# Split weight tiles in two phases of 128 bytes, in a hybrid decoder trunk in float32

## The chip, the cores and the metric

The kernel runs on one core of one Trainium2 chip, as one program in one launch. The metric is the time of one execution in microseconds (us). The core has a matrix engine (TensorE, "PE" in the profile, with its weight loads shown apart as "PEld"), a vector engine (VectorE, DVE), a scalar engine (ScalarE, ACT), GpSimd (POOL), a queue processor (SyncE, SP) that issues most of the loads, 128 partitions of on-chip memory in which every tile lives, and eight accumulator banks that TensorE writes.

## The reference

Two layers act on 256 rows of width 1024. Each layer is a half-step FFN, a token mixer beside four memory cross-attention heads, and another half-step FFN. The mixer of layer 0 is a chunkwise mLSTM, that of layer 1 a sliding-window attention.

```python
def swiglu(x, w_in, w_out):
    gate, up = jnp.split(x @ w_in, 2, axis=-1)
    return (jax.nn.silu(gate) * up) @ w_out
...
    mem_kv = rms_norm(mem, mem_norm_g) @ mem_w_kv
...
    for i in range(DEPTH):
        j = i // N_MIXERS
        x = x + 0.5 * swiglu(rms_norm(x, ffn1_norm_g[i]), ffn1_w_in[i], ffn1_w_out[i])
        hn = rms_norm(x, mix_norm_g[i])
        if i % N_MIXERS == 0:
            proj = hn @ a_w_in[j]
            y_tok = mlstm_heads(proj[..., :A_TOK], a_gate_b[j], a_h_norm_g[j])
...
        y_mem = memory_heads(xq, mem_k, mem_v, xa_q_norm_g[i], xa_k_norm_g[i])
        x = x + jnp.concatenate([y_tok, y_mem], axis=-1) @ w_out
        x = x + 0.5 * swiglu(rms_norm(x, ffn2_norm_g[i]), ffn2_w_in[i], ffn2_w_out[i])
    return x
```

D_MODEL is 1024, the FFN's inner width 2816. All is float32, and nearly all the work is in the products with the weights.

## The kernel before

**Products in three parts.** Each weight tile and each activation is split into a high part, rounded to the matmul's float32r, and the low part that is left over. A product is then three matmuls into one accumulator bank: high by high, high by low, low by high (`mm3`, line 449). All of them go through the helper `mm` (line 445), so that the profile shows nearly every matmul on line 446. Each is 128 by 128 weights against 256 moving columns.

**The weight stream.** The class `Stream` (line 266) brings the weights in the order of one long plan, tile after tile, 349 of them. Tile i goes through three steps. `fetch` issues the load into a raw tile `wr`, `round` (line 290) has ScalarE copy it to the high tile `wh` in float32r (line 300), and `rest` (line 303) has VectorE subtract to get the low tile `wl` (line 315). TensorE takes a tile with `take` and gives it back with `drop`. Most tiles are 128 partitions by 1024 elements, 4096 bytes in a partition. The tile pools are rings: `wrp` has 5 buffers, `whp` and `wlp` have 8 each, so tile i reuses the buffer of tile i - 8.

**The stages.** `program()` runs `memory`, `ffn`, `mixer_a`, `ffn`, `ffn`, `mixer_b`, `ffn`. One FFN has 11 groups of four weight tiles for its inner columns, and 24 tiles for its output; a tile serves 24 matmuls, and the FFN has 1,584. In its first part the moving operands are `xh` and `xl`, the split activations; in the second they are tiles `u`, the split hidden columns. The weights are the stationary operand there. Some projections of the mixers (groups with `rows=True`) do it the other way: `xh` and `xl` are stationary, and `wh` and `wl` move. `Norm.finish` (line 527) sums the squares of a row with two matmuls on the constant tile `onesr` (four, on a norm with `rows=False`); they stand on line 446 too, between the matmuls of the next stage. Transposes (line 460) and the small products of the heads (lines 455, 1366, 1371, 1422) interrupt the stream only in the mixers.

**The order.** It is written out while the program is built: `Weave` keeps a clock for each engine and decides when each step is issued. No address enters into it.

**Addresses.** The pools lie one behind the other in a partition, in the order in which they are made, and a pool takes the size of its tiles. The constants of `cst` come first, so the first pool behind them, `xhp`, begins at byte 29,632. From the sizes follow these places (bytes in a partition) and their phase, the place modulo 512; every tile in a ring and every slice that a matmul takes lies a multiple of 512 bytes further:

| tiles | first byte | modulo 512 |
|---|---|---|
| `onesr` | 16,512 | 128 |
| `xh`, `xl` | 29,632 and 37,824 | 448 |
| `u` | 46,016 | 448 |
| `wr` | 113,664 | 0 |
| `wh` | 134,144 | 0 |
| `wl` | 166,912 | 0 |
| `t` | 199,680 | 0 |

In what follows, the distance of a matmul is the place of its stationary operand less that of its moving one, modulo 512. It is (0 - 448) = 64 for all matmuls on weight tiles in the FFNs and output projections, 448 - 0 = 448 for the row-wise groups, 128 - 448 = 192 for `Norm.finish` with `onesr` stationary, and 448 - 128 = 320 where `onesr` moves. The low tile of a weight lies 32,768 bytes behind its high tile.

Of the kernel before, what the change touches and what calls it, by code (L numbers as in the profile page):

```python
# [10 lines left out]
F32 = mybir.dt.float32  # L11
F32R = mybir.dt.float32r
# [7 lines left out]
P = 128  # L20
# [120 lines left out]
def tile_trunk(ctx: ExitStack, tc: tile.TileContext, a, out):  # L141
# [3 lines left out]
    def mk(pool, shape, dt, tag):  # L145
        seq[0] += 1
        return pool.tile(shape, dt, tag=tag, name=f"{tag}_{seq[0]}")

    def pool(name, bufs, **kw):
        return ctx.enter_context(tc.tile_pool(name=name, bufs=bufs, **kw))  # L150

    cst = pool("cst", 1)
    onesr = mk(cst, [P, T], F32R, "onesr")
    nc.vector.memset(onesr.bitcast(F32), 1.0 / D)
    wv = Weave()


    xhp = pool("xhp", 4)
# [1 line left out]
    up = pool("up", 31)  # L160
    vp = pool("vp", 2)
    wrp = pool("wrp", 5)
    whp = pool("whp", 8)
    wlp = pool("wlp", 8)
    tp = pool("tp", 8)
    sp = pool("sp", 2)
    gp = pool("gp", 1)
    cp = pool("cp", 24)
    pbs = [pool(f"pb{i}", 1, space=PSUM) for i in range(8)]

    tt = nc.vector.tensor_tensor
# [56 lines left out]
    maskd = con[:, C_MASK:C_MASK + T]  # L228
    ones = mk(cst, [P, 1], F32, "ones")
    nc.vector.memset(ones, 1.0)  # L230
    mhalf = mk(cst, [P, 16], F32, "mhalf")
    nc.vector.memset(mhalf, -0.5)
    warm = mk(cst, [P, 1], F32, "warm")
    act(warm, ones, AF.Silu)
# [31 lines left out]
    class Stream:  # L266
# [23 lines left out]
        def round(self, i):  # L290
            shape, j = self.plan[i][1], Job(wv, self.landed[i])
            gates = shape[2] == 8
            n = 1024 if gates else shape[1] * shape[2]
            self.hi[i] = mk(whp, [P, 8, P] if gates else shape, F32R, "wh")
            if gates:
                nc.gpsimd.memset(self.hi[i].bitcast(F32), 0.0)
                for s in range(2):
                    nc.scalar.copy(self.hi[i][:, :, s * 32:s * 32 + 4], self.raw[i][:, :, s * 4:s * 4 + 4])
            else:
                nc.scalar.copy(self.hi[i], self.raw[i])  # L300
            self.cast[i] = j.act(n)

        def rest(self, i):
            shape, j = self.plan[i][1], Job(wv, self.cast[i])
            gates = shape[2] == 8
            self.lo[i] = mk(wlp, [P, 8, P] if gates else shape, F32R, "wl")
            if gates:
                nc.gpsimd.memset(self.lo[i].bitcast(F32), 0.0)
                for s in range(2):
                    d = slice(s * 32, s * 32 + 4)  # L310
                    tt(out=self.lo[i][:, :, d], in0=self.raw[i][:, :, s * 4:s * 4 + 4],
                       in1=self.hi[i][:, :, d].bitcast(F32), op=ALU.subtract)
                j.dve(64)
            else:
                tt(out=self.lo[i], in0=self.raw[i], in1=self.hi[i].bitcast(F32), op=ALU.subtract)  # L315
                j.dve(shape[1] * shape[2])
            self.subbed[i] = j.t
# [100 lines left out]
    def mixer_plan(w, pair, rest, w_out, gates=None):  # L418
        for kh in range(2):
            for c0 in pair:  # L420
                yield cols(w, c0, kh)
        for c0 in rest:
            if c0 == gates:
                yield chunks(w)[:, :, c0:c0 + 8], [P, 8, 8], None
                continue
            for kh in range(2):
                yield cols(w, c0, kh)
        for kc in ORDER + LATE:
            yield row(w_out, kc)
# [1069 lines left out]
```

## Time and profile before

| | |
|---|---|
| three timed runs | 1007.48, 1008.93, 1001.01 us; median 1007.48 |
| the profiled execution | 1016.15 us |
| its span, first to last instruction | 1014.3 us |
| granted TensorE clock, mean | 0.997 |
| moved by the DMA engines | 182.72 MB, mean 180 GB/s |

The page's span is the time between the first and the last instruction of one execution; the execution's own time is 1.85 us longer. The profiled execution is the longest of the four. Busy times are sums over one engine. A matmul's recorded duration is modelled, and the next one starts before it ends: what the engine does per unit of time is read from the starts, or from the number of matmuls in a window.

### The profile page before, as it was taken

The numbers are of one execution on the slowest core, as the hardware profiler recorded it, in microseconds if no ns is written. First come the engines' busy times: TensorE is split into PE (matmuls) and PEld (weight loads), VectorE is DVE, ScalarE is ACT, GpSimd is POOL, SyncE is SP. The second block draws the span as 40 slices with busy tenths as digits, with TensorE's granted clock in tenths as the row PEclk, the third lists the DMA queues.
The fourth block names the chain that finished last, engine by engine and source line by source line (L and its number), as shares of the span: only waits on it lengthen the run. The fifth ranks groups of instructions, "written<-read, shape, count | busy, mean of one in ns | idle before, by whom it ended". The sixth has DMA issues, their size and how long they took to land.

```text
span 1014.3 us, 20574 instructions
## 1 busy us (share of the span) xinstructions
PE 1004.9 (99%) x8554; PEld 989.9 (98%) x8554; DVE 677.9 (67%) x1096; ACT 512.9 (51%) x774; POOL 56.9 (6%) x46
## 2 busy tenths in 40 slices
PE   8999999999999999999999999999999999999998
PEld 7999999999999999999999999999998899999998
DVE  6985565668766596655567667665778778666551
ACT  6754453456556465444444445354566665453440
POOL 1400000010101000000010000000111010000000
PEclk9999999999999999999999999999999999999999
DMA  8876545656454666665656665656622347656650
GB/s 287 251 230 201 192 157 179 205 154 191 124 183 141 191 187 195 196 205 165 199 165 183 212 209 168 194 191 190 214 85 83 102 150 246 211 176 203 200 170 23
DMA packets 171614, 182.72 MB, mean 180 GB/s; under 512 B 7196, under 2 KB 165328, under 8 KB 171520
## 3 DMA queue, kind: packets, MB, share of 16 engines
q1 hardware_dynamic: 170384, 179.60, 56.3%
q8 instruction: 67, 1.10, 0.4%
q0 software_dynamic: 416, 0.75, 0.4%
q10 hardware_dynamic: 720, 1.05, 0.3%
q14 instruction: 27, 0.22, 0.1%
HBM read 180.32 MB, written 1.05 MB: 179 GB/s over the span
## 4 chain that ended last, share of the span: by engine, by line
PE 98%; DMA 1%; DVE 0%; SPq 0%; ACT 0%; issue 0%; DVEq 0%
PE bank L446 93%; PE bank L455 2%; PE bank L460 2%; DMA wr<-in_mem_w_kv_dram 1%; PE bank L1371 1%; PE bank L1422 1%; PE bank L1366 0%; ACT wh L300 0%; SPq L376 0%; DVE t L865 0%; DVE wl L315 0%; DVE t L866 0%; SPq L287 0%; DVEq L315 0%
## 5 line engine op out<-in xcount | busy, mean ns | idle before, releaser
L315 DVE TENSOR_TENSOR wl<-wr,wh 128x1024 fp32r<-128x1024 f32 (+2 forms) x349 | 407.3, 1206 | 52.9 <-ACT wh L300 52.2
L446 PE MATMUL bank<-xh,wh 128*128 128x256 f32 x1544 | 431.6, 280 | 0.0
L446 PE MATMUL bank<-xh,wl 128*128 128x256 f32 x1544 | 430.6, 279 | 0.0
L446 PE MATMUL bank<-xl,wh 128*128 128x256 f32 x1544 | 430.6, 279 | 0.0
L300 ACT CAST wh<-wr 128x1024 fp32r<-128x1024 f32 (+2 forms) x349 | 341.0, 1020 | 77.7 <-PE bank L446 53.1
L446 PE MATMUL bank<-u,wh 128*128 128x256 f32 x1792 | 313.0, 280 | 0.0
L446 PEld LDWEIGHTS bank<-xh,wh 128*128 128x128 f32 x1544 | 291.6, 189 | 0.1
L446 PEld LDWEIGHTS bank<-xh,wl 128*128 128x128 f32 x1544 | 291.6, 189 | 0.0
L446 PEld LDWEIGHTS bank<-xl,wh 128*128 128x128 f32 x1544 | 290.0, 188 | 0.1
L446 PEld LDWEIGHTS bank<-u,wh 128*128 128x128 f32 x1792 | 271.9, 188 | 1.7 <-issue 1.7
L446 PE MATMUL bank<-u,wl 128*128 128x256 f32 x896 | 249.9, 279 | 0.0
L446 PEld LDWEIGHTS bank<-u,wl 128*128 128x128 f32 x896 | 169.2, 189 | 0.0
L797 ACT ACTIVATE t<-t 128x512 f32<-128x512 f32 x44 | 27.8, 632 | 192.2 <-DVE t L794 191.8
L794 DVE TENSOR_TENSOR t<-bank,rb 128x256 f32<-128x256 f32 x88 | 36.7, 424 | 86.2 <-PE bank L446 86.2
L446 PE MATMUL bank<-wh,xh 128*128 128x256 f32 x208 | 60.0, 289 | 0.0
L520 POOL TENSOR_TENSOR u<-u,t 128x512 f32<-128x512 f32 x14 | 24.5, 1750 | 606.0 <-ACT t L517 605.8
L494 ACT ACTIVATE xh<-u,gcol 128x256 fp32r<-128x256 f32 x48 | 21.7, 502 | 72.5 <-DVE u L847 59.9
L446 PE MATMUL bank<-wl,xh 128*128 128x256 f32 x208 | 57.9, 279 | 0.0
L446 PE MATMUL bank<-wh,xl 128*128 128x256 f32 x208 | 57.9, 278 | 0.0
L844 DVE TENSOR_TENSOR t<-bank,hrb 128x512 f32<-128x512 f32 x15 | 10.4, 691 | 64.3 <-PE bank L446 64.3
L800 DVE TENSOR_TENSOR t<-t,bank 128x256 f32<-128x256 f32 x88 | 33.1, 418 | 27.0 <-ACT t L797 26.9
L466 DVE TENSOR_TENSOR u<-t,u 128x512 fp32r<-128x512 f32 x44 | 30.4, 692 | 28.2 <-ACT u L464 28.2
(189 smaller groups left out, 657.4 us busy)
## 6 DMA issues: line engine op xcount, KB each, us to landing
wr<-in_ffn_w_in_dram SPq DMA_DIRECT2D x176, 512.0 KB, 5.0
wr<-in_ffn_w_out_dram SPq DMA_DIRECT2D x80, 512.0 KB, 4.9
wr<-in_a_w_in_dram SPq DMA_DIRECT2D x28, 512.0 KB, 4.5
wr<-in_b_w_in_dram SPq DMA_DIRECT2D x14, 512.0 KB, 4.9
wr<-in_a_w_out_dram SPq DMA_DIRECT2D x12, 512.0 KB, 4.3
wr<-in_b_w_out_dram SPq DMA_DIRECT2D x12, 512.0 KB, 3.2
wr<-in_ffn_w_out_dram SPq DMA_DIRECT2D x16, 256.0 KB, 2.6
wr<-in_mem_w_kv_dram SPq DMA_DIRECT2D x6, 512.0 KB, 8.0
```

What stands on the lines that cost most here:

```text
L300: nc.scalar.copy(self.hi[i], self.raw[i])
L315: tt(out=self.lo[i], in0=self.raw[i], in1=self.hi[i].bitcast(F32), op=ALU.subtract)
L446: nc.tensor.matmul(ps, lhsT, rhs, start=start, stop=stop, skip_group_check=True)
L455: nc.tensor.matmul(ps, lhsT, rhs, start=start, stop=stop, skip_group_check=True)
L460: nc.tensor.transpose(ps, src, ident[:k, :k])
L466: tt(out=lo, in0=src, in1=hi.bitcast(F32), op=ALU.subtract)
L494: act(hi[:, m], xn[:, m], AF.Copy, scale=g(self.gi + 2 * c2 + m))
L520: nc.gpsimd.tensor_tensor(out=self.acc, in0=self.acc, in1=sq, op=ALU.add)
L794: tt(out=t[:, m], in0=bs[m].t[:, :T], in1=x.rb, op=ALU.mult)
L797: act(t, t, AF.Silu)
L800: tt(out=t[:, m], in0=t[:, m], in1=bs[m].t[:, T:], op=ALU.mult)
L844: tt(out=t, in0=halves(b.t), in1=pair(x.hrb), op=ALU.mult)
```

## The change

The ring of eight high tiles becomes two rings of four, and so does the ring of eight low tiles. Tile i goes to ring i modulo 2. Between the first and the second pair of rings the pool `gp` is put, which held one tile of 64 bytes (`acol`) and now also holds `mhalf`, another 64 bytes: together 128. `mhalf`, a constant that GpSimd's power operations read (line 473), leaves the constants for that, and a tile `pad` of the same size is put among them, so that the pools behind them begin where they did.

```diff
     wv = Weave()
+    mk(cst, [P, 16], F32, "pad")
...
-    whp = pool("whp", 8)
-    wlp = pool("wlp", 8)
+
+    whp, wlp = [pool("whp0", 4)], [pool("wlp0", 4)]
+    gp = pool("gp", 1)
+    whp.append(pool("whp1", 4))
+    wlp.append(pool("wlp1", 4))
     tp = pool("tp", 8)
     sp = pool("sp", 2)
-    gp = pool("gp", 1)
     cp = pool("cp", 24)
+    mhalf = mk(gp, [P, 16], F32, "mhalf")
...
-    mhalf = mk(cst, [P, 16], F32, "mhalf")
...
-            self.hi[i] = mk(whp, [P, 8, P] if gates else shape, F32R, "wh")
+            self.hi[i] = mk(whp[i % 2], [P, 8, P] if gates else shape, F32R, f"wh{i % 2}")
...
-            self.lo[i] = mk(wlp, [P, 8, P] if gates else shape, F32R, "wl")
+            self.lo[i] = mk(wlp[i % 2], [P, 8, P] if gates else shape, F32R, f"wl{i % 2}")
```

The places after it, from the sizes:

| tiles | first byte | modulo 512 |
|---|---|---|
| `wh0`, `wl0` (even tiles) | 134,144 and 150,528 | 0 |
| `mhalf`, `acol` | 166,912 and 166,976 | |
| `wh1`, `wl1` (odd tiles) | 167,040 and 183,424 | 128 |
| `t` | 199,808 | 128 |

`onesr`, `xh`, `xl`, `u` and `wr` stay where they were; some small constants move by 64 bytes, and `t` and the small pools behind it by 128 (`cp`, the last, by 64). A tile is still reused after eight. For an odd tile the distance is 192 in place of 64, and 320 in place of 448 in the row-wise groups; for an even tile it is as before. A low tile lies 16,384 bytes behind its high tile. Of the program's matmuls in float32r, about half work on odd tiles.

## The prediction

> **What bounds the kernel now.** I read the page first: the span, the busy shares, the granted clock and the chain of work that ended last.
>
> ```profile
> span 1014.3 us, 20574 instructions
> PE 1004.9 (99%) x8554; PEld 989.9 (98%) x8554; DVE 677.9 (67%) x1096; ACT 512.9 (51%) x774; POOL 56.9 (6%) x46
> PEclk9999999999999999999999999999999999999999
> PE 98%; DMA 1%; DVE 0%; SPq 0%; ACT 0%; issue 0%; DVEq 0%
> L315 DVE TENSOR_TENSOR wl<-wr,wh 128x1024 fp32r<-128x1024 f32 (+2 forms) x349 | 407.3, 1206 | 52.9 <-ACT wh L300 52.2
> L300 ACT CAST wh<-wr 128x1024 fp32r<-128x1024 f32 (+2 forms) x349 | 341.0, 1020 | 77.7 <-PE bank L446 53.1
> ```
>
> TensorE is 98% of the chain, at full clock. The cast and the subtraction that split a weight tile take 1.02 and 1.21 us on two engines that are 51% and 67% busy, so they stand off the path. What counts is the rate at which TensorE takes matmuls. A matmul's own duration does not tell it, since neighbours overlap; the distance from start to start, which I call the pitch, does. So I asked next how many matmuls of line 446 (the helper `mm`) fall into the whole span and into the four FFNs (columns: window, its length, TensorE busy and matmuls, weight loads, granted clock, DMA share, GB/s):
>
> ```profile
> 0.00:1014.30 1014.30, 956.59 (x8154) 948.21 (x8154) 1.00 0.57 180
> 49.60:228.20 178.60, 178.60 (x1518) 178.60 (x1518) 1.00 0.61 188
> 362.00:547.80 185.80, 185.80 (x1579) 185.80 (x1579) 1.00 0.62 193
> 548.20:727.50 179.30, 179.30 (x1585) 179.30 (x1584) 1.00 0.62 193
> 838.10:1009.00 170.90, 170.90 (x1511) 170.90 (x1510) 1.00 0.57 179
> ```
>
> The second and third FFN run the same code on the same shapes at the same clock and DMA share, yet one takes 185.8 us for 1,579 matmuls and the other 179.3 us for 1,585. The view of one line, cut to a stretch inside the first, second, third and fourth FFN, shows it again (one kind of matmul, every third of the stream; durations min/median/max, first and last start):
>
> ```profile
> L446 PE MATMUL bank<-xh,wh x279: 280/281/282, 59.7 to 158.0; 128*128 128x256 f32 x140
> L446 PE MATMUL bank<-xh,wh x306: 280/281/282, 369.7 to 477.5; 128*128 128x256 f32 x153
> L446 PE MATMUL bank<-xh,wh x295: 275/276/277, 560.0 to 659.9; 128*128 128x256 f32 x148
> L446 PE MATMUL bank<-xh,wh x293: 275/276/277, 849.8 to 949.1; 128*128 128x256 f32 x147
> ```
>
> (158.0 − 59.7) us / 278 / 3 = 117.9 ns and (477.5 − 369.7) / 305 / 3 = 117.8 ns; (659.9 − 560.0) / 294 / 3 = 113.3 ns and (949.1 − 849.8) / 292 / 3 = 113.4 ns. There are two pitches, a long one of 117.8 and a short one of 113.3, 4.5 ns apart, and a stage keeps the one it begins with from its first tile to its last. Weight loads show the same two cases (first FFN, then third):
>
> ```profile
> L446 PEld LDWEIGHTS bank<-xh,wh x278: 191/192/193, 60.0 to 157.8; 128*128 128x128 f32 x139
> L446 PEld LDWEIGHTS bank<-xh,wh x295: 187/188/188, 559.9 to 659.8; 128*128 128x128 f32 x148
> ```
>
> Under the long pitch one load of three lasts 192 ns, under the short one all last 188.
>
> **What one pitch or the other is worth.** Counting in the timeline from start to start, 4,103 of the 8,112 neighbouring pairs of line 446 stand at 116 to 126 ns: the two FFNs above (3,097) and about a thousand in the opening and the mixers. 4,103 × 4.5 ns = 18.5 us. The profiled execution took 1016.15 us (span 1014.3 and 1.85 around it), so with the short pitch throughout it would be 997.7 us, and with the long one throughout 997.7 + 8,154 × 4.5 ns = 1034.4 us. On this scale the three timed runs hold about 9% (1001.01), 27% (1007.48) and 31% (1008.93) of long pitch, the profiled one 50%; one whole FFN is 1,584 × 4.5 ns = 7.1 us, about the step between the timed runs. I take it, as an estimate, that the runs of before differ by which stages fell into which pitch.
>
> **What sets the pitch.** The trace has a few places where the address distance between weights and moving operand changes without a pause. In an FFN the moving tiles stand at 448 and the weights at 0 in 512 bytes, a distance of 64. The sum of squares (`Norm.finish`, two matmuls on `onesr`, which stands at 128) sits between FFN tiles and makes it 192 for two matmuls: exactly the distance that the odd tiles get after the change. The timeline of TensorE at the end of the second FFN, and at the start of that same FFN (start us, duration, matmul):
>
> ```profile
> 547.70 0.28 PE L446 MATMUL bank<-xh,wl 128*128 128x256 f32 x1
> 547.82 0.40 PE L446 MATMUL bank<-u,onesr 128*128 128x256 f32 x2
> 548.06 0.28 PE L446 MATMUL bank<-xh,wh 128*128 128x256 f32 x1
> 548.17 0.28 PE L446 MATMUL bank<-xl,wh 128*128 128x256 f32 x1
> 548.29 0.28 PE L446 MATMUL bank<-xh,wl 128*128 128x256 f32 x1
> 548.40 0.28 PE L446 MATMUL bank<-xh,wh 128*128 128x256 f32 x1
> ```
> ```profile
> 361.44 0.28 PE L446 MATMUL bank<-xl,wh 128*128 128x256 f32 x1
> 361.55 0.28 PE L446 MATMUL bank<-xh,wl 128*128 128x256 f32 x1
> 361.67 0.46 PE L446 MATMUL bank<-u,onesr 128*128 128x256 f32 x2
> 361.96 0.28 PE L446 MATMUL bank<-xh,wh 128*128 128x256 f32 x1
> 362.08 0.28 PE L446 MATMUL bank<-xl,wh 128*128 128x256 f32 x1
> 362.20 0.28 PE L446 MATMUL bank<-xh,wl 128*128 128x256 f32 x1
> ```
>
> In the first, long pitch comes in and short pitch leaves, for the whole third FFN. In the second, short comes in (0.11 apart) and long leaves (0.12), for the whole second FFN. The timeline has the first kind four times (at 46, 228, 548 and 838 us) and the second once, there with a pause of some 60 ns inside. So a trip 64, 192, 64 turned the pitch over in five cases of five. The row-wise projections of the mixers, whose moving operand is the weight tile, stand at 448, and 320 on `onesr`; there are two more turns:
>
> ```profile
> 727.47 0.28 PE L446 MATMUL bank<-wh,xl 128*128 128x256 f32 x1
> 727.58 0.64 PE L446 MATMUL bank<-onesr,u 128*128 128x256 f32 x4
> 728.05 0.28 PE L446 MATMUL bank<-wh,xh 128*128 128x256 f32 x1
> 728.17 0.28 PE L446 MATMUL bank<-wl,xh 128*128 128x256 f32 x1
> ```
> ```profile
> 256.85 0.28 PE L446 MATMUL bank<-wh,xl 128*128 128x256 f32 x1
> 256.96 0.28 PE L446 MATMUL bank<-xh,wh 128*128 128x256 f32 x1
> 257.08 0.28 PE L446 MATMUL bank<-xl,wh 128*128 128x256 f32 x1
> 257.20 0.28 PE L446 MATMUL bank<-xh,wl 128*128 128x256 f32 x1
> ```
>
> From 448 to 320, short becomes long at once; from 448 to 64 too. What neither trace nor code shows is a long stretch at 192 or 320.
>
> **The change part by part.** It adds and removes no instruction: engine by engine the two programs have the same operations, shapes and waits in the same order, and each split tile is still reused after eight. Moving `mhalf` changes where 31 small POOL operations read; POOL is 6% busy: nothing. Casts and subtractions may run at other speeds at the new addresses: 1.02 and 1.21 us against the 24 × 113.3 ns = 2.7 us that a tile occupies TensorE hide any change short of a doubling. What is left is the pitch. The distance now changes at nearly every tile, some 350 times (349 tiles, by the rows of lines 300 and 315), and stays for 24 matmuls.
>
> The price of a change: from 547.70 to 548.17 the two changes around `onesr` take 0.47 us for four pitches, which at 113.3 ns would be 0.453; 17 ns, or about 9 for each. Changes that start from the short pitch show next to none (361.44, 361.55, 361.67). Between nothing and 9 ns, 350 changes cost 0 to 3.2 us; I take 2, since half of them would be of either kind.
>
> [...]
>
> **My forecast** is the turning seen five times in five, carried on: each visit to an odd tile and back turns the pitch over, whichever half of it does so. Then half of the 8,154 matmuls run at either pitch, whatever a stage begins with: 997.7 + 4,077 × 4.5 ns = 1016.0, and 2 for the changes: 1018 us, with its own range of 1013 (40% long, no price) to 1023 (60%, 3 us).
>
> **The rivals.**
> - *It settles short.* If 192 and 64 both hold the short pitch once it is there, every stage falls into it within a few tiles and stays: 997.7 plus 0 to 3, so 1000 us, not slower than before. For it: all four long arrivals left short. Against it: 361.55 to 362.08, though the pause there may have done it, not the distance. It decides from the first odd tile entered at 113 ns: if that tile stays at 113, this is the case.
> - *It settles long.* If the odd tiles hold the long pitch and give it on, as 320 did at 728.05 (long came in, long stayed): 1034 and 2, say 1028 to 1037.
> - *The change does nothing that it says.* If pauses, not distances, turn the pitch, and `onesr` turned it by its wait for the sums, stages fall as before: 1001 to 1016, 1007.5 in the middle. 361.67 is for it, 256.96 against it. [...]
> - *A third, still shorter pitch at 192.* Nothing shows one. If the odd half gained as much again as the two known pitches differ, 997.7 − 4,077 × 4.5 ns = 979; 979 to 997.
>
> **How the numbers follow.** Chances: turning 0.45, short 0.22, long 0.13, nothing 0.14, third pitch 0.06. The predicted time is the first, 1018 us. The range of 999 to 1034 leaves out the third pitch, a part of the short case and half of the long: about 0.2. One per cent either way of 1007.48, about what a measurement of this kernel can tell from no change, is 997.4 to 1017.6. Faster: the third pitch alone, 0.06. Slower: the long case and some 60% of the turning case, 0.13 + 0.27 = 0.40. Within: the rest, 0.54. So the likeliest single time lies at the edge of the band: the change decides whether a run is an average of the two pitches or a lucky draw, and before's median is a lucky one, at 27%.
>
> **What would show each step.** Windows inside an FFN give the number of matmuls: 140 us hold 1,191 at the long pitch and 1,238 at the short, and 1,214 or so if it turns. The timeline at a tile's edge shows whether turns come every second tile, and whether 192 itself is long or short. Weight loads of 192 ns come and go with the long stretches. Times of single runs should lie closer together than the 8 us of before, since no stage keeps a draw. I am wrong if whole FFNs still run at one pitch, or if a stretch shows a pitch that is neither 113.3 nor 117.8.

## The result, and the profile after

Over 20 runs the changed kernel took 1000.06 us in the median (999.17 to 1001.84). The kernel before, in 20 runs beside it, took 1007.5 (1000.14 to 1023.55). The ratio is 0.9954 with a 95% interval of 0.9935 to 0.9972. This ratio, like those further down, leaves out runs more than 1.5% above a kernel's fastest; here those are before's three runs at 1021 to 1024, by the prediction's scale its runs with the most long pitch, so the medians of all runs stand further apart, at 0.9926. Before spreads over 23 us, the changed kernel over less than 3.

The page of the changed kernel (profiled execution 1001.35 us; casts and subtractions now stand on lines 303 and 318, `mm` on 449):

```profile
span 999.6 us, 20574 instructions
PE 991.2 (99%) x8554; PEld 976.6 (98%) x8554; DVE 677.3 (68%) x1096; ACT 511.0 (51%) x774; POOL 56.7 (6%) x46
PE 98%; DMA 1%; ACT 0%; DVE 0%; issue 0%; SPq 0%; DVEq 0%; ACTq 0%
L318 DVE TENSOR_TENSOR wl<-wr,wh 128x1024 fp32r<-128x1024 f32 (+2 forms) x349 | 407.0, 1204 | 51.9 <-ACT wh L303 50.5
L303 ACT CAST wh<-wr 128x1024 fp32r<-128x1024 f32 (+2 forms) x349 | 339.0, 1019 | 74.4 <-PE bank L449 48.9
```

The instructions are as many as before, and the cast and the subtraction last as long to within 2 ns. The chain is TensorE's, 98% of it. What differs is how closely matmuls follow. The windows of `mm` inside the four FFNs (window, its length, TensorE busy and matmuls, weight loads, granted clock, DMA share, GB/s), first of the changed kernel, then of the profiled execution of before:

```profile
60.00:200.00 140.00, 140.00 (x1238) 140.00 (x1237) 1.00 0.64 200
370.00:510.00 140.00, 140.00 (x1238) 140.00 (x1237) 1.00 0.64 199
560.00:700.00 140.00, 140.00 (x1238) 140.00 (x1237) 1.00 0.61 189
850.00:990.00 140.00, 140.00 (x1238) 140.00 (x1237) 1.00 0.54 171
```
```profile
60.00:200.00 140.00, 140.00 (x1191) 140.00 (x1190) 1.00 0.60 190
370.00:510.00 140.00, 140.00 (x1191) 140.00 (x1190) 1.00 0.62 197
560.00:700.00 140.00, 140.00 (x1238) 140.00 (x1237) 1.00 0.61 192
850.00:990.00 140.00, 140.00 (x1238) 140.00 (x1237) 1.00 0.63 200
```

All four FFNs now run at the short pitch, where before had two at the long one. Counted from start to start in the timeline, 884 pairs still stand at 116 to 126 ns (before: 4,103). They cost 3.95 us over the short pitch, and 1001.35 − 3.95 = 997.4 us, where before's profile gave 1016.15 − 18.3 = 997.8. So, to within 0.4 us, the difference between the two profiled executions is the number of long pairs.

The timeline shows how the long pitch leaves. TensorE around the second FFN's `onesr`, in the changed kernel (start us, duration, matmul):

```profile
354.48 0.28 PE L449 MATMUL bank<-xh,wl 128*128 128x256 f32 x1
354.59 0.44 PE L449 MATMUL bank<-u,onesr 128*128 128x256 f32 x2
354.87 0.28 PE L449 MATMUL bank<-xh,wh 128*128 128x256 f32 x1
...
357.58 0.28 PE L449 MATMUL bank<-xh,wl 128*128 128x256 f32 x1
357.69 0.28 PE L449 MATMUL bank<-xh,wh 128*128 128x256 f32 x1
...
358.05 0.28 PE L449 MATMUL bank<-xh,wh 128*128 128x256 f32 x1
358.17 0.28 PE L449 MATMUL bank<-xl,wh 128*128 128x256 f32 x1
358.28 0.28 PE L449 MATMUL bank<-xh,wl 128*128 128x256 f32 x1
```

The two matmuls on `onesr` take 354.87 − 354.59 = 0.28 us, some 50 ns more than two pitches, so there is a pause in them. Behind it the pitch is long, (357.58 − 354.87) / 23 = 117.8 ns. It ends with the tile: from 358.05 on, 3,095 matmuls in a row follow at 113.3 ns, up to 708.8 us, over more than a hundred changes of distance and across the next `onesr`. Here the first change away from a long pitch ended it, and until 708.8 us none brought it back.

### The profile page after: what moved, and what is told of

It is laid out like the page before. It is cut to its first block, busy times and chain, and to the rows that moved or that the text cites. A ratio compares the mean times of both kernels' runs of the same rounds, so it can differ in the third digit from the quotient of the medians.

```text
span 999.6 us, 20574 instructions
## 1 busy us (share of the span) xinstructions
PE 991.2 (99%) x8554; PEld 976.6 (98%) x8554; DVE 677.3 (68%) x1096; ACT 511.0 (51%) x774; POOL 56.7 (6%) x46
## 4 chain that ended last, share of the span: by engine, by line
PE 98%; DMA 1%; ACT 0%; DVE 0%; issue 0%; SPq 0%; DVEq 0%; ACTq 0%
PE bank L449 93%; PE bank L458 2%; PE bank L463 2%; DMA wr<-in_mem_w_kv_dram 1%; PE bank L1374 1%; PE bank L1425 1%; PE bank L1369 0%; DMA u<-in_memT_dram 0%; ACT wh L303 0%; ACT u L709 0%; DVE wl L318 0%; DVE t L868 0%; DVE t L869 0%; SPq L379 0%; DVE u L711 0%
## 5 line engine op out<-in xcount | busy, mean ns | idle before, releaser
L318 DVE TENSOR_TENSOR wl<-wr,wh 128x1024 fp32r<-128x1024 f32 (+2 forms) x349 | 407.0, 1204 | 51.9 <-ACT wh L303 50.5
L303 ACT CAST wh<-wr 128x1024 fp32r<-128x1024 f32 (+2 forms) x349 | 339.0, 1019 | 74.4 <-PE bank L449 48.9
L449 PE MATMUL bank<-u,wh 128*128 128x256 f32 x1792 | 307.9, 277 | 0.0
```

The costliest lines, as they stand in the source:

```text
L449: nc.tensor.matmul(ps, lhsT, rhs, start=start, stop=stop, skip_group_check=True)
```

## The experiments

Each experiment is the kernel before with one edit, and computes the whole reference. The expectations were written in four groups, each ahead of its runs, and the theories in them changed from group to group, as the text behind each tells. "Distance" is used as above. Each group ran on a chip of its own with before beside it, and before's median differs between them (1006.7 to 1015.2 us); whether by what its runs drew alone, or by the chip too, isn't shown.

**Is 192 a good distance by itself?** `e1_all128` puts all split tiles 128 bytes further, so that every FFN matmul stands at 192 and nothing alternates (row-wise groups at 320).

```diff
+    mk(pool("lead", 1), [P, 32], F32, "lead")
     whp = pool("whp", 8)
```

> All sixteen split tiles stand 128 bytes further, so the distance in the FFNs is 192 throughout and never changes within a stage (onesr, at 128, then makes it 192 to 192: no change either). Theory A, the change of distance is what ends the long pitch and a constant distance keeps whichever pitch comes in: single runs spread over 7 us or more as those of before do (1000 to 1024), and the profile has whole FFNs at one pitch, the long one (1191 matmuls in 140 us) among them in this or another run. Rival B, 192 is itself a distance at which only the short pitch holds: all runs at 999 to 1003, every FFN at 1238 matmuls in 140 us.

It took 1028.54 us (6 runs, 1028.01 to 1030.6); before, beside it, 1008.79; ratio 1.023 [1.0191, 1.0269]. The first of its windows (the other three hold 1,191 too):

```profile
60.00:200.00 140.00, 140.00 (x1191) 140.00 (x1190) 1.00 0.61 193
...
```

All four FFNs are long in the profile, and the six runs lie within 2.6 us of one another, so they seem to be long in every run; neither theory had foreseen that. `onesr` stands at 192 too, so here a norm changes nothing, and long stayed long at all four norms of the FFNs. So the gain doesn't come from the places of the odd tiles: those same places, used for all tiles, cost 2%.

**Is it the split into two rings?** `e2_rings0` has the two rings of four without the 128 bytes between them: distance 64 for all tiles, low tiles 16,384 bytes behind the high ones as after the change.

```diff
-    whp = pool("whp", 8)
-    wlp = pool("wlp", 8)
+    whp, wlp = [pool("whp0", 4)], [pool("wlp0", 4)]
+    whp.append(pool("whp1", 4))
+    wlp.append(pool("wlp1", 4))
...
-            self.hi[i] = mk(whp, [P, 8, P] if gates else shape, F32R, "wh")
+            self.hi[i] = mk(whp[i % 2], [P, 8, P] if gates else shape, F32R, f"wh{i % 2}")
```

> Two rings of four for high and for low tiles as in the change, the low tile 16384 bytes behind the high one, but no 128 bytes between them, so the distance is 64 for all tiles. Theory A: as before, runs from 1000 to 1024, spread over 7 us or more, whole FFNs at one pitch. Rival C, the new layout of the rings (the nearer low tile) brings the gain: 999 to 1003, all FFNs short.

1007.75 us (12 runs, 1000.96 to 1022.5), ratio 1.0004 [0.9974, 1.0035], with before's spread. The rings do nothing; the 128 bytes do it.

**Does a stage belong to a pitch?** `e3_again` is the kernel before, unchanged, profiled once more.

> The kernel before once more, for a second profile of it. Theory A: the runs of before differ by which FFNs fell into which pitch, so this profile has another set of long and short FFNs than the first one (long, long, short, short for the four), and its time is 998 us plus 4.45 ns for each long pair. If the pitch went with the place in the program (rival D, each FFN has its own pitch by its addresses), the same two would be long again.

1008.54 us (12 runs, 1000.89 to 1016.51), ratio 1.0001 [0.9969, 1.0034]; its profiled execution took 1003.26. The first two FFNs, long in the first profile of the same program, are short here:

```profile
60.00:200.00 140.00, 140.00 (x1238) 140.00 (x1237) 1.00 0.64 201
370.00:510.00 140.00, 140.00 (x1238) 140.00 (x1237) 1.00 0.64 200
...
```

So the pitch of these stages is drawn in each execution; neither the code nor its addresses alone settle it. In this profile the norms at 222.50 and 535.02 us have short before them and short behind them: the trip 64, 192, 64 does not turn a short pitch.

**Does any change of distance do it?** `e4_alt64` is the change with a gap of 64 bytes: distances 64 and 128 by turns.

```diff
+    whp, wlp = [pool("whp0", 4)], [pool("wlp0", 4)]
+    mk(pool("gap", 1), [P, 16], F32, "gap")
+    whp.append(pool("whp1", 4))
+    wlp.append(pool("wlp1", 4))
```

> Odd tiles 64 bytes further in place of 128: the distance goes 64, 128, 64 in the FFNs. Theory A, any change of distance will do: 999 to 1003 with little spread. If the step has to be 128 (rival E, only 192 against 64 ends the long pitch): runs from 1000 to 1024, with long FFNs.

1022.11 us (6 runs, 1020.64 to 1023.52), ratio 1.0162 [1.0127, 1.0197]. The timeline alternates: on even tiles it settles at 113.3 ns behind the first three matmuls, on odd ones it stays uneven, mostly near 119.5 with about one matmul in five at 115, 118.3 in the mean.

```profile
103.22 0.28 PE L448 MATMUL bank<-xl,wh 128*128 128x256 f32 x1
103.34 0.28 PE L448 MATMUL bank<-xh,wl 128*128 128x256 f32 x1
103.46 0.28 PE L448 MATMUL bank<-xh,wh 128*128 128x256 f32 x1
103.58 0.28 PE L448 MATMUL bank<-xl,wh 128*128 128x256 f32 x1
...
105.24 0.28 PE L448 MATMUL bank<-xh,wh 128*128 128x256 f32 x1
105.35 0.28 PE L448 MATMUL bank<-xl,wh 128*128 128x256 f32 x1
105.47 0.28 PE L448 MATMUL bank<-xh,wl 128*128 128x256 f32 x1
```

A distance seems to have a price of its own, then, and 128 to be a dear one (the table below has it alone). From here on I held this theory: at 64 and at 192 both pitches can last, a pause draws one of them, and a change between 64 and 192 without a pause ends the long one and leaves the short one alone.

**How few changes are enough?** `e5_eighth128` keeps seven tiles of eight at 64 and puts one at 192.

```diff
+    whp, wlp = [pool("whp0", 7)], [pool("wlp0", 7)]
+    mk(pool("gap", 1), [P, 32], F32, "gap")
+    whp.append(pool("whp1", 1))
+    wlp.append(pool("wlp1", 1))
...
+            self.hi[i] = mk(whp[i % 8 == 7], [P, 8, P] if gates else shape, F32R, f"wh{int(i % 8 == 7)}")
```

> Seven buffers of eight at distance 64, the eighth at 192: a trip 64, 192, 64 every eight tiles, with no pause in it. Theory A2 (both pitches last at 64 and at 192 as long as the distance stays; a change of distance turns long into short and leaves short alone): every FFN goes short within at most eight tiles, some 0.9 us after its start, 999 to 1004 with little spread. The turning of the prediction (a trip turns the pitch over, whatever it was): long and short alternate every eight tiles, half of the FFN matmuls are long, 1012 to 1020.

1001.89 us (12 runs, 999.67 to 1002.63), where before had 1015.2 beside it (1000.29 to 1023.3); ratio 0.9915 [0.9879, 0.9952]. In its profile all four windows hold 1,238 matmuls, the first FFN is short for 1,649 in a row, and 3,163 in a row follow later. The second window:

```profile
...
370.00:510.00 140.00, 140.00 (x1238) 140.00 (x1237) 1.00 0.63 200
...
```

If each visit turned the pitch over, whole blocks of tiles in the FFNs would have been long; there is none. For the FFNs, the turning of the prediction is refuted.

**The reverse of it.** `e6_eighth64` starts from the 1028.5 us of `e1_all128`: seven tiles of eight at 192, and one at 64.

```diff
+    mk(pool("lead", 1), [P, 32], F32, "lead")
+    whp, wlp = [pool("whp0", 7)], [pool("wlp0", 7)]
+    mk(pool("gap", 1), [P, 96], F32, "gap")
+    whp.append(pool("whp1", 1))
+    wlp.append(pool("wlp1", 1))
```

> Seven buffers of eight at 192, the eighth at 64. With all at 192 every FFN was long from first to last matmul (1028). Theory A2: one tile in eight is enough, since the change takes the long pitch away and the short one lasts at 192 too: FFNs short, 996 to 1004; the row-wise groups, now mostly at 320, run mostly short as they did with all at 192, so rather below the change itself. Rival F, long is what 192 brings by itself within a few tiles: the FFNs are long for seven tiles of eight, about 1024.

1003.29 us (12 runs, 1001.42 to 1004.86), ratio 0.9923 [0.9888, 0.9959]. One tile in eight at another distance takes away 25 of the 28 us that a constant 192 costs over 1000. The timeline of its second FFN, where a long stretch ends (a visit to 64 begins with the matmul at 387.26):

```profile
386.68 0.28 PE L449 MATMUL bank<-xl,wh 128*128 128x256 f32 x1
...
387.15 0.28 PE L449 MATMUL bank<-xh,wl 128*128 128x256 f32 x1
387.26 0.28 PE L449 MATMUL bank<-xh,wh 128*128 128x256 f32 x1
387.38 0.28 PE L449 MATMUL bank<-xl,wh 128*128 128x256 f32 x1
387.49 0.28 PE L449 MATMUL bank<-xh,wl 128*128 128x256 f32 x1
```

387.15 − 386.68 is 0.47 us for four pitches, and 387.49 − 387.15 is 0.34 for three. The pause at 353 us had drawn long for 287 matmuls; 2,811 short ones follow. Since 287 are twelve tiles, one earlier visit had come and gone without ending it: a change usually ends a long pitch, but not always the first.

The timelines of the changed kernel, `e5_eighth128` and `e6_eighth64` together give the count, for changes between 64 and 192 on stationary weights with no pause in the seven pairs ahead. Short came in 491 times and stayed short 491 times. Long came in 17 times; it was ended 11 times and went on 6 times.

**Distance or place?** `e7_xmoved` leaves the weights where they were and moves the activations, so that the FFN distance is 192 with `wh` at phase 0. The norms become trips 192, 320, 192.

```diff
+    mk(pool("lead", 1), [P, 96], F32, "lead")
     xhp = pool("xhp", 4)
...
+    mk(pool("gap", 1), [P, 32], F32, "gap")
     wrp = pool("wrp", 5)
```

> The activations xh, xl, u and v stand 384 bytes further and the weights where they were, so the distance is 192 throughout with weights at phase 0. If the distance decides: as with all weights at 128, every FFN long, 1026 to 1031 with little spread (the norms now make 192, 320, 192, which may end the long pitch in a stage). If the weights' own place decides (or their place against wr): as before, 1000 to 1024 with spread.

1020.13 us (12 runs, 1013.26 to 1023.05), ratio 1.0091 [1.0048, 1.0135]: below the 1026 to 1031 expected. The windows tell why:

```profile
...
370.00:510.00 140.00, 140.00 (x1191) 140.00 (x1190) 1.00 0.61 192
560.00:700.00 140.00, 140.00 (x1238) 140.00 (x1237) 1.00 0.61 193
850.00:990.00 140.00, 140.00 (x1238) 140.00 (x1237) 1.00 0.61 194
```

FFNs that begin behind a pause are long, as in `e1_all128`; those that begin behind a norm's trip, at 545.39 and 835.18 us, are short, and stay short over a whole FFN at 192. So 192 can hold either pitch. None of the 12 runs lies below 1013, where 14 of before's 35 lie below 1010. That, and the long FFNs behind a pause, speak for the distance, whichever operand is moved, and against the weights' own place. I had given the norms a passing remark in the expectation, and no place in its range.

**A change that is none.** `e8_alt256` has a gap of 256 bytes ([P, 64] in the diff of `e4_alt64`): 64 and 320 by turns.

> Odd tiles 256 bytes further: 64, 320, 64 in the FFNs, 448 and 192 in the row-wise groups. Alternating by 64 (64, 128) ended whole-stage pitches too, but its odd tiles at 128 ran at 118 to 119 ns and its even ones at 113. Theory A2 has the even tiles short again; the odd ones are short if 320 has a short pitch for stationary weights (999 to 1003) and some 118 if it has none (1015 to 1022).

1012.07 us (12 runs, 1000.6 to 1023.49), ratio 1.002 [0.9969, 1.0071]: before's spread is back, and two whole FFNs are long across every tile edge, with 1,579 long matmuls in a row behind the pause at 361.87. I had expected it to act like the change.

```profile
60.00:200.00 140.00, 140.00 (x1191) 140.00 (x1191) 1.00 0.60 189
370.00:510.00 140.00, 140.00 (x1191) 140.00 (x1191) 1.00 0.62 197
...
```

64 and 320 act as one distance in the FFNs: by these runs it goes modulo 256. In the row-wise groups too, 448 and 192 by turns leave the pitch as it is (23 such changes without a pause, 17 with long and 6 with short coming in). By that count 448 is a 192, and 320 is a 64.

**Three more constant distances.** `e9_dist0`, `e10_dist128` and `e12_dist32` are `e1_all128` with a lead of [P, 48], [P, 16] and [P, 56]: distances 256, 128 and 288, so 0, 128 and 32 modulo 256 (that 256 and 288 act as 0 and 32 would is taken over from 64 and 320; in no kernel here do weight tiles stand at 0 or 32).

> All split tiles stand 192 bytes further: distance 256, which is 0 modulo 256, in the FFNs and in the row-wise groups, never changing but at the norms. It fills in the map: 64 alone takes either pitch after a pause, 192 alone takes the long one, 128 ran at 118 to 119 ns. Theory P (the distance counts modulo 256, and each distance has its own pitch after a pause): runs close together or in steps of 7 us, no value known; if 0 holds the short pitch, FFNs and row-wise groups both run short and the time is 997 to 999, below every version so far; if 0 is the worst, as two reads that want the same place at once would make it, over 1030.

> All split tiles stand 64 bytes further: distance 128 in the FFNs, 384 (128 modulo 256) in the row-wise groups. In the kernel with 64 and 128 by turns the odd tiles, at 128, ran at four intervals of 119.5 and one of 115, 118.7 ns in the mean. If that is what 128 is by itself: all stages at 118 to 119 ns, 997 plus 8154 times 5.4 ns, so 1034 to 1043. If it was only the alternation: runs as before, 1000 to 1024, or at the long pitch throughout, 1028 to 1034.

> All split tiles 224 bytes further: 288 in the FFNs, 32 modulo 256, and 224 in the row-wise groups, constant. It lies between 0 (120.0 ns, 1051 us) and 64 (113.3 or 117.8). If only a distance that is a multiple of 128 brings the third pitch: 1000 to 1031 with one of the two known pitches in each stage. If the pitch worsens with nearness to 0: 118 to 120 ns, 1034 to 1050. If there is a distance that is short by itself, this could be it: 997 to 1000, both in FFNs and in row-wise groups, below the change.

One window of `e9_dist0`, two of `e10_dist128` and one of `e12_dist32`:

```profile
60.00:200.00 140.00, 140.00 (x1169) 140.00 (x1168) 1.00 0.60 187
```
```profile
60.00:200.00 140.00, 140.00 (x1182) 140.00 (x1181) 1.00 0.60 188
370.00:510.00 140.00, 140.00 (x1169) 140.00 (x1168) 1.00 0.61 190
```
```profile
60.00:200.00 140.00, 140.00 (x1185) 140.00 (x1185) 1.00 0.60 188
```

At 0 and 128 the times fall into the ranges given for the dearest case, and 32 into that for nearness to 0. With the kernels above this gives a table (the pitch read from starts in an FFN):

| constant distance, modulo 256 | kernel | pitch, ns | time, us | ratio to before |
|---|---|---|---|---|
| 0 | `e9_dist0` | 120.0 | 1050.72 | 1.0443 [1.0376, 1.0510] |
| 32 | `e12_dist32` | 118.3 | 1036.02 | 1.0291 [1.0258, 1.0325] |
| 64 | before | 113.3 or 117.8 | 1000 to 1024 | |
| 128 | `e10_dist128` | 115 to 123; mean 118.7 in three FFNs, 120.0 in the second | 1041.71 | 1.0357 [1.0303, 1.0411] |
| 192 | `e1_all128`, `e7_xmoved` | 117.8, or 113.3 if it comes in short | 1028.54 and 1020.13 | 1.023 and 1.0091 |

None of those at 0, 32 and 128 shows an FFN at 113.3. At these three only the weights were moved, so only at 192 is the distance told from the weights' own place.

**Pause or distance at the one turn to long?** `e11_nopause` is before with the planner's clock set 0.8 us later ahead of the norm's matmuls, so that they are issued later among the tile's and their sums are there when TensorE comes to them. No distance changes.

```diff
             yield from split_plain(j, acc[:, 0], sums[:, 0], sums[:, 1], T)
+            j.t += 0.8
             yield from room(j, 1, first=True)
```

> The kernel before, with the two norm matmuls on onesr recorded 0.8 us later on the planner's clock, so that both halves of the sums are there when TensorE comes to them. Theory A3 (a pause draws the pitch anew, a change of distance without a pause takes long away and leaves short alone): the second FFN, whose norm had the pause of some 60 ns in every profile so far, now always begins short; the first can still be long, since it starts behind the transposes of the memory keys. Runs at about 1000 to 1009, none of the 1014 to 1024 that before has in a third of its runs; the norms show short to short or long to short. Turning (the prediction's step): the second FFN turns as the norms come, runs at 1000 to 1024.

1008.76 us (12 runs, 1007.72 to 1010.99), ratio 1.0038 [1.0016, 1.006]. The timeline at the place where the prediction saw short turn to long (361.67 us there):

```profile
361.63 0.28 PE L446 MATMUL bank<-xl,wh 128*128 128x256 f32 x1
361.74 0.28 PE L446 MATMUL bank<-xh,wl 128*128 128x256 f32 x1
361.86 0.39 PE L446 MATMUL bank<-u,onesr 128*128 128x256 f32 x2
362.08 0.28 PE L446 MATMUL bank<-xh,wh 128*128 128x256 f32 x1
362.19 0.28 PE L446 MATMUL bank<-xl,wh 128*128 128x256 f32 x1
362.31 0.28 PE L446 MATMUL bank<-xh,wl 128*128 128x256 f32 x1
```

The two matmuls on `onesr` now take 0.22 us, two short pitches; in before's profile they took 0.29. The distance goes 64, 192, 64 as it did there, and short leaves: the place lies inside 3,470 short matmuls in a row, from 327.40 to 720.67 us.

```profile
60.00:200.00 140.00, 140.00 (x1191) 140.00 (x1190) 1.00 0.62 192
370.00:510.00 140.00, 140.00 (x1238) 140.00 (x1237) 1.00 0.63 200
...
```

The runs don't decide it. The twelve lie within 3.3 us and none reaches 1014, as the theory expects, but none of before's 17 runs beside them does either (1000.1 to 1009.38). None of the twelve comes near 1000: the first FFN, which starts behind the memory's transposes, was long in the profile, and its 1,584 matmuls at 4.5 ns are 7.1 us, the step from 1001 to 1008.

## Why the prediction was wrong

The bound and the sizes held. TensorE's rate is all that moved. The two pitches are 113.3 and 117.8 ns in every profile at 64 and 192; the base of 997.7 us, worked out from before alone, came out as 997.4 in the changed kernel. The 1,238 matmuls in 140 us are the count that was given for the short pitch. That runs of before differ by what their stages fell into, an estimate then, is shown by `e3_again` for two profiles of one program. Casts, subtractions and the moved `mhalf` cost nothing, as costed (1019 and 1204 ns). The price of a change of distance was put at 0 to 3.2 us for 350 of them, taken as 2: with 997.4 us left after the long pairs are taken off, there is no room for it, so it is about 0. In the changed kernel's timeline, the 325 pairs across a change between 64 and 192 to which short comes in, without a pause, average 113.3 ns. The 17 ns that the prediction read around `onesr` at 547.82 are about what four pairs at the long pitch bring, 4 × 4.5 = 18, since the long pitch was still ending there.

The step that failed is the turning: "a trip 64, 192, 64 turned the pitch over in five cases of five". Four of the five were alike: long came in, short left, without a pause. The fifth, at 361.67 us, was the only one from short to long, and the prediction noted "a pause of some 60 ns inside" and still counted it as a turn by distance. `e11_nopause` took the pause away from that place and short stayed. One such case would not settle it, since with the pause, too, the place came out short in two profiles of four. Five such trips without a pause that began short are now seen at a constant 64 (222.50 and 535.02 in `e3_again`, 539.37 in `e2_rings0`, 361.86 and 540.92 in `e11_nopause`), and all five stayed short, as did all 491 tile edges counted above. The pause at the second FFN's norm led to long in before and `e8_alt256` and to short in `e3_again` and `e2_rings0` (in the latter 1,237 matmuls in the 140 us from 370 us on, but the first five pairs behind the pause, from 360.51 us, still took 0.59 us, the long pitch; what ended it there, at a constant 64, isn't shown). So in the FFNs the distance doesn't turn the pitch over; it only ends the long one (11 of 17 times at a given change), and a pause draws afresh.

This holds where the weights are the stationary operand on both sides. The prediction's two other turns, at 256.96 and 727.58, are of another kind, and further profiles show them again. At the first the weights pass from moving to stationary operand, which the prediction read as a change of distance alone, from 448 to 64; short turned long there without a pause in `e2_rings0`, `e3_again`, `e8_alt256` and `e11_nopause` again, while in `e1_all128`, where the distance goes from 320 to 192, short stayed (255.76). The second, in a row-wise group, turned the same way in these four and in `e5_eighth128`, and stayed short in `e1_all128`, where all stands at 320 (734.05). In the row-wise groups of the changed kernel, short turned long at 9 of 9 changes of distance without a pause. So the turning exists, but not in the FFNs, where most of the matmuls are; the prediction carried it over to them from a case with a pause. What sets the two kinds apart was not tested.

What happened is the first rival, "it settles short", priced at 1000 us and given 0.22. Its test, whether the first odd tile entered at 113 ns stays at 113, came out for it: 1,649 short matmuls in a row from 49.09 us in the first FFN. The evidence against it that the prediction named, 361.55 to 362.08, came with its own answer ("the pause there may have done it"), and should have lost its weight there: without it, no trip 64, 192, 64 had turned short to long.

"It settles long" had a true part. 192 does hold the long pitch when a stage begins with it (`e1_all128`, 28 us). In the FFNs of the changed kernel's profile it gets that chance for one tile at a time, at 354.87 and again behind the norm at 822.81. "The change does nothing" had one too, since pauses do draw the pitch; but a gap of 256 bytes undoes the gain (`e8_alt256`, 1012.07 us), and one of 128 makes it (1000.06), so the distance is in it. No profile here shows a third, shorter pitch at 192.

The forecast of a narrow spread was right for another reason than the one given: not because each run averages the two pitches, but because a long pitch that a pause draws in an FFN is soon cut off, both times at the next tile edge in the changed kernel's profile.

The 3.95 us that remain sit mostly in the row-wise groups (549 of the 884 long pairs, with the norms inside them), which stand at 192 and 64 modulo 256 by turns. Without the norms it is 540 pairs, against 536 in before's profile: the change gained nothing there. The timeline of the changed kernel in one of them:

```profile
717.66 0.28 PE L449 MATMUL bank<-wh,xh 128*128 128x256 f32 x1
...
719.67 0.28 PE L449 MATMUL bank<-wh,xl 128*128 128x256 f32 x1
...
720.72 0.28 PE L449 MATMUL bank<-wh,xl 128*128 128x256 f32 x1
...
722.42 0.28 PE L449 MATMUL bank<-wh,xl 128*128 128x256 f32 x1
```

(719.67 − 717.66) / 17 = 118 ns on one tile and (722.42 − 720.72) / 15 = 113 on the next: here the pitch turns from tile to tile, much as the prediction expected of the FFNs. Keeping these groups at 320 throughout might save up to 549 × 4.5 ns = 2.5 us, an estimate; it wasn't tried by itself. In `e1_all128`, where they stand at 320, only 76 such pairs are long, but in `e6_eighth64`, at 320 for seven tiles of eight, 401 are. No kernel of this study was faster than the changed one; `e5_eighth128` and `e6_eighth64` came within some 3 us of it.

What stays open is the mechanism beneath: whether two accesses meet, and which, and why 256 bytes are the period. The runs give the map, not its cause.

## What to carry to other kernels

When executions of one program differ by steps of a stage's worth at full clock (7 us here), count the matmuls in equal windows of like stages, in two profiles of the same program, before reading any edit into a difference. A stream of matmuls can be held at a slower pitch (here 117.8 to 120.0 ns in place of 113.3) by the distance of its two operands' addresses and by a chance pause; changing that distance now and then was a cheap way out here (one tile in eight took 1028.5 us to 1003.3), but only between distances that both allow the fast pitch (64 and 192; 64 and 128 by turns took 1022.1 us), and only where the weights stay the stationary operand. And when a pattern is counted from few cases, the one that carries the doubtful half of it is to be looked at alone: four arrivals of one kind and one of the other, with a pause in it, are not five of five.

## What the runs showed of the hardware

At the same instructions and a full clock (1.00 in every window above), the pitch went from 113.3 to 120.0 ns and the time from 1000 to 1050.7 us (`e9_dist0`) with nothing but the places of tiles moved; the table above has them by the distance of the stationary from the moving operand, modulo 256 bytes.

At two of these distances, 64 and 192, the pitch has two lasting values, 113.3 and 117.8 ns. It kept what it had over thousands of matmuls (3,095 in a row in the changed kernel, 1,581 long pairs in before), and a pause of 50 to 65 ns could switch it: behind some 65 ns lost at one norm (361.67 us) the rest of an FFN of before's profile stayed long, 7 us longer than a short one. The pause at that norm didn't always do so: the FFN behind it was short in `e3_again` (1,238 matmuls in 140 us), and but for its start in `e2_rings0` (0.29 us for the norm's two matmuls, then 1,237 in 140 us).
